# Attention of a hybrid block by whole patches: a ring for probabilities, four paired tables, first loads off ScalarE, output stored by patches

## The chip, the cores and the metric

The kernel runs on one core of a Trainium2 chip. The metric is the device time in microseconds; each kernel is run several times and the median is taken. TensorE (PE) multiplies matrices from SBUF into PSUM, VectorE (DVE), ScalarE (ACT) and GpSimd (POOL) work on tiles of 128 partitions, and loads and stores are DMA transfers. They are issued from the instruction queues of ScalarE, GpSimd and SyncE (SP); an engine that issues one is occupied for that time.

## The reference

One layer of a trunk: x of 2048 positions (a grid of 32 rows by 64 columns) and 1024 channels is normalised, shifted and scaled, projected once (`h @ w_in + b_in`) and split between two head groups; their outputs are concatenated and projected back.

```python
na_out = neighbourhood_attention(na_q, na_k, na_v, rpb) * jax.nn.silu(na_z)
...
ml_out = hm * jax.nn.silu(ml_z)
return jnp.concatenate([na_out, ml_out], axis=-1) @ w_out
...
h_res = h_res + gate[:, None, :] * y
return rmsnorm(h_res, final_norm_w).astype(x.dtype)
```

Neighbourhood attention has 8 heads of 64 channels. Each position of the grid attends to a window of 8 rows by 16 columns of keys, clipped at the border; a table of relative positions is added to the scores and keys outside the window are masked. The second group is an mLSTM of 4 heads in both directions; only its result is read by the part that the change touches. Everything is float32; matmuls are done as three products of high and low parts (hi x hi, lo x hi, hi x lo).

## The kernel before

The program has three stretches: the projection and convolution, then the passes of the mLSTM with the remaining column blocks of the projection as filler (matmuls into `pq`, L1046), and from about 930 us on the attention with the output projection. The last stretch is what the change touches. There PE's order is written out by hand: slots are emitted one after the other, and between their parts `pump(n)` takes n matmuls from a queue of filler, first the last `pq`, then the output projection (`y`, L1626) of a finished patch.

The grid is cut into 16 patches of 8 rows by 16 columns (128 queries). A unit is a patch and one channel block `ct` of two heads, so there are 64 units. A slot of the kernel before takes a pair of units: `scores` multiplies their queries by the keys of the patch's window (264 to 480 keys) into four PSUM banks (`pS`, L1538), adds the table and takes the row's minimum on VectorE (`mn`, L1546; the signs are turned), and ScalarE takes the exponential and its sum (L1547). `values` then multiplies the transposed probabilities of the pair in the slot before by the values (`pO`, L1581). `normalised` divides by the sums on VectorE (L1558). `turned` transposes on PE, in three or four pieces per head (`pT`, L1566, one PSUM buffer), and ScalarE copies the result to SBUF (`pt`, L1568), four times per slot. Fillers stand in front of the first and behind each transposition: 6, 5, 5, 4, 4 matmuls (8, 7, 7, 7, 7 in the first three slots).

When both pairs of a patch are through, its attention output, gated with z, and the mLSTM's part are split into a high and a low part for the output projection: `mixed` calls `mix_high` (a ScalarE copy, L1596) and `mix_low` (a VectorE subtraction, L1601), first for the mLSTM's half, then for the attention's. This is done in every other slot, behind the second and third transposition. The finished halves of y are added to the residual x on VectorE (L1631), squared and summed on ScalarE (L1633), and after a reciprocal root the row is scaled (L1668) and stored (L1669, issued from GpSimd). ScalarE and VectorE work strictly in the order of emission.

Loads: value rows of a patch (`v`, L1466, one DMA per grid row), z (L1476), the mLSTM's part (`wlo_a`/`whi_a`, L1483) and x (L1493) are issued from GpSimd; q (L1448), the tables (`tab`, L1510) and weights from SyncE. Of the first patch, v, z, the mLSTM's part and the third q are issued from ScalarE. There are two table tiles; the order of units within a patch is turned so that a table that fits the next patch too isn't loaded again. Probabilities live in four tiles (`pbuf`), transposed ones in four others (`pt`).

Of the kernel before, what the change touches and what calls it, by code (L numbers as in the profile page):

```python
# [58 lines left out]
class Kernel:  # L59
# [965 lines left out]
    def nq_gen(self):  # L1025
# [66 lines left out]
        while late:  # L1092
            nc.scalar.dma_start(*late.pop(0))
# [152 lines left out]
    def ml_pass2(self, ml, h):  # L1246
# [11 lines left out]
        def load_z(gi):  # L1258
            while ("mz", h, gi) not in self.zdone:
                self.pump(1)  # L1260
            if h == MH - 1 and gi == NG - 1:
                t = self.p2.tile([P, 4, P], F32, tag="pt", bufs=4, name="zt_last")
            else:
                t = self.mle.tile([P, 4, CH], F32, tag="zt", bufs=1, name=f"zt_{h}_{gi}")
# [134 lines left out]
    def phase2(self):  # L1399
# [23 lines left out]
        og = self.out[0].rearrange("(r c) d -> r c d", c=GRID_W)  # L1423
# [4 lines left out]
        qs = [p.tile([P, 2, 2, P], F32R, name=f"qs{i}") for i in range(3)]  # L1428
# [8 lines left out]
        units = []  # L1437
        for b in patches:
            again = units and kind(b) == kind(units[-1][0])
            order = range(4) if not units or not (again == (units[-1][1] == 3)) else range(3, -1, -1)  # L1440
            units += [(b, ct) for ct in order]
        NU = len(units)

        def load_q(i):
            if 2 * i >= NU:
                return
            b, c0 = units[2 * i][0], min(units[2 * i][1], units[2 * i + 1][1])
            (nc.gpsimd, nc.gpsimd, nc.scalar, nc.sync)[min(i, 3)].dma_start(qs[i % 3].bitcast(F32), self.d_qna[c0 // 2, b])  # L1448
# [48 lines left out]
        tabs = [p.tile([P, 960], F32, name=f"tab{i}") for i in range(2)]  # L1497
        place, follows, user = [], {}, {}
        for u, (b, ct) in enumerate(units):
            same = [w for w in (u - 1, u - 3) if w >= 0 and units[w][1] == ct and units[w][0] != b and kind(units[w][0]) == kind(b)]  # L1500
            place.append(place[same[0]] if same else (1 - place[u - 1] if u else 0))
            if not same:
                follows[user.get(place[u], -1 - place[u])] = u
            user[place[u]] = u

        def load_tab(u):
            b, ct = units[u]
            nk = geo[b][4]
            src = self.d_t[PR_T[b // 4]][PC_T[b % 4]][ct].rearrange("q e k -> q (e k)")
            (nc.gpsimd if u < 2 else nc.sync).dma_start(tabs[place[u]][:, : 2 * nk], src)  # L1510
# [11 lines left out]
        U = {}  # L1522

        def scores(pair):
            made = {}
            for u in pair:
                b, ct = units[u]
                pr, pc, nr, nkc, nk, rpc, nch = geo[b]
                q, c = qs[(u // 2) % 3], ct % 2
# [4 lines left out]
                for n, (e, f) in enumerate(((0, 0), (1, 0), (0, 1))):  # L1534
                    for j, ps in enumerate(made[u]):
                        js = slice(j * HD, (j + 1) * HD)
                        o = ps.rearrange("p (r c) -> p r c", c=nkc)
                        nc.tensor.matmul(o, q[js, e, c, :], keys[f][js], start=(n == 0), stop=(n == 2))  # L1538
            for u in pair:
                nk = geo[units[u][0]][4]  # L1540
                pts = []
                sums = few.tile([P, 2], F32, tag="sums", bufs=3, name=f"sums_{u}")
                for j, ps in enumerate(made[u]):
                    pt = pbuf[(2 * u + j) % 4]
                    mn = few.tile([P, 1], F32, tag="mn", bufs=4, name=f"mn_{u}_{j}")
                    nc.vector.tensor_tensor_reduce(pt[:, :nk], ps, tabs[place[u]][:, j * nk : (j + 1) * nk], 1.0, 3e38, ALU.add, ALU.min, mn)  # L1546
                    nc.scalar.activation(pt[:, :nk], pt[:, :nk], AF.Exp, bias=mn, scale=-1.0, accum_out=sums[:, j : j + 1])  # L1547
                    pts.append(pt)
                if u in follows:
                    load_tab(follows[u])  # L1550
# [10 lines left out]
        def turned(u, j):  # L1561
# [5 lines left out]
            t = p.tile([P, 4, P], F32, tag="pt", bufs=4, name=f"pt_{u}_{j}")  # L1567
# [3 lines left out]
        def values(pair):  # L1571
            po = pO.tile([P, 2, P], F32, tag="pO", name=f"pO_{pair[0]}")
            for u in pair:
# [3 lines left out]
                for i in range(nch):  # L1577
                    v, n = L[b]["v"][i]
                    for j in range(2):
                        h = 2 * ct + j  # L1580
                        nc.tensor.matmul(po[j * HD : (j + 1) * HD, ct % 2, :], v[:n, h * HD : (h + 1) * HD], pt[j][:n, i, :], start=(i == 0), stop=(i == nch - 1))  # L1581
            return po

        def gated(pair, po):
            b, ct = units[pair[0]]
            c0 = ct // 2 * 2
# [154 lines left out]
        def slot(m):  # L1741
            new = (2 * m, 2 * m + 1) if 2 * m < NU else ()
            old = (2 * m - 2, 2 * m - 1) if m else ()
            if m:
                load_q(m + 2)
# [139 lines left out]
```

## Time and profile before

| what | value |
|---|---|
| median of the runs shown | 1314.05 us (1313.41 to 1314.33) |
| profiled execution, its own time | 1315.58 us |
| its span, first to last instruction | 1313.8 us |
| PE busy | 1282.8 us, 98% |
| VectorE, ScalarE, GpSimd busy | 793.4, 531.3 and 260.6 us |
| first matmul of scores | about 950 us |
| last stores issued | 1306.04 and 1306.26 us |

The busy time of PE is modelled from pipelined records: a matmul that is shown 0.40 us long can be followed by the next one after 0.23 us. What PE spends is therefore read from start to start. In rows of the timeline stand the start, the duration, engine, line, operation, output and inputs, shapes and the number of records in a run, and in brackets how long the engine had been idle and what released it. In rows of waits stand who waited at which line for what, the sum in us, the number of times and the longest one. An engine name with a q is its queue, issuing a DMA.

### The profile page before, as it was taken

The numbers are of one execution on the slowest core, as the hardware profiler recorded it, in microseconds if no ns is written. First come the engines' busy times: TensorE is split into PE (matmuls) and PEld (weight loads), VectorE is DVE, ScalarE is ACT, GpSimd is POOL, SyncE is SP. The second block draws the span as 40 slices with busy tenths as digits, with TensorE's granted clock in tenths as the row PEclk, the third lists the DMA queues.
The fourth block names the chain that finished last, engine by engine and source line by source line (L and its number), as shares of the span: only waits on it lengthen the run. The fifth ranks groups of instructions, "written<-read, shape, count | busy, mean of one in ns | idle before, by whom it ended". The sixth has DMA issues, their size and how long they took to land.

```text
span 1313.8 us, 23067 instructions
## 1 busy us (share of the span) xinstructions
PE 1282.8 (98%) x8170; PEld 1103.1 (84%) x8170; DVE 793.4 (60%) x2394; ACT 531.3 (40%) x1172; POOL 260.6 (20%) x380
## 2 busy tenths in 40 slices
PE   9889999999999999999999999999999999999996
PEld 8889999999888887888888888888777778778785
DVE  5876452112567565166678878767447576766663
ACT  4444243542234222223323323333256555565551
POOL 1400002432000000111212002122305423324431
PEclk7989999999999999999999999999999999999998
DMA  9799955997778764645756767656678756656651
GB/s 363 250 282 305 262 188 152 228 234 202 195 183 186 170 149 110 193 131 165 207 153 209 245 184 215 214 157 183 206 252 261 203 182 194 209 181 194 190 178 48
DMA packets 220662, 263.31 MB, mean 200 GB/s; under 512 B 25463, under 2 KB 165623, under 8 KB 220548
## 3 DMA queue, kind: packets, MB, share of 16 engines
q1 hardware_dynamic: 142526, 189.92, 50.1%
q10 hardware_dynamic: 63270, 35.75, 9.6%
q0 software_dynamic: 14752, 36.17, 9.4%
q8 instruction: 65, 1.06, 0.3%
q14 instruction: 49, 0.40, 0.1%
HBM read 177.28 MB, written 92.72 MB: 206 GB/s over the span
## 4 chain that ended last, share of the span: by engine, by line
PE 80%; issue 4%; DVE 3%; DMA 3%; ACT 1%; POOL 1%; POOLq 0%; ACTq 0%; SPq 0%; DVEq 0%
PE pq L1046 23%; PE y L1626 11%; PE pc L605 4%; PE pc L606 4%; PE pc L604 4%; PE pO L1581 3%; PE pT L1566 3%; PE pvo L604 3%; PE pvo L606 3%; PE pvo L605 3%; PE pS L1538 2%; PE pv L606 2%; PE pv L605 2%; PE pv L604 2%; PE pi L1285 2%
## 5 line engine op out<-in xcount | busy, mean ns | idle before, releaser
L1046 PE MATMUL pq<-hhi,whi_a 128*128 128x512 f32 x512 | 208.4, 407 | 0.9 <-ACT u L951 0.9
L1046 PE MATMUL pq<-hlo,whi_a 128*128 128x512 f32 x512 | 208.2, 407 | 0.0
L1046 PE MATMUL pq<-hhi,wlo_a 128*128 128x512 f32 x512 | 206.7, 404 | 0.0
L1046 PEld LDWEIGHTS pq<-hhi,whi_a 128*128 128x128 f32 x512 | 96.8, 189 | 17.5 <-ACT u L951 1.3
L1046 PEld LDWEIGHTS pq<-hhi,wlo_a 128*128 128x128 f32 x512 | 96.7, 189 | 16.9 <-POOL wlo_a L1020 0.4
L1046 PEld LDWEIGHTS pq<-hlo,whi_a 128*128 128x128 f32 x512 | 96.8, 189 | 16.1 <-issue 0.5
L1020 POOL TENSOR_TENSOR wlo_a<-rawq,whi_a 128x1024 fp32r<-128x1024 f32 x19 | 45.6, 2399 | 293.3 <-ACT whi_a L1019 281.6
L1568 ACT ACTIVATE pt<-pT 96x384 f32<-96x384 f32 (+3 forms) x128 | 65.8, 514 | 87.3 <-PE pT L1566 85.1
L1547 ACT ACTIVATE pbuf<-pbuf,mn 128x480 f32<-128x480 f32 (+5 forms) x128 | 75.9, 594 | 47.8 <-DVE mn L1546 47.8
L1626 PE MATMUL y<-hhi,whi_a 128*128 128x512 f32 x256 | 91.6, 420 | 0.5 <-ACT whi_a L1596 0.5
L1626 PE MATMUL y<-hhi,wlo_a 128*128 128x512 f32 (+1 forms) x272 | 90.6, 399 | 0.2 <-ACT y L1633 0.2
L1466 POOL DMA_DIRECT2D v<-d_vna x158 | 81.8, 523 | 45.0 <-PE pO L1581 17.0
L1288 ACT ACTIVATE num<-px,gtile 128x129 f32<-128x129 f32 x120 | 38.3, 366 | 113.1 <-PE px L1283 80.4
L1546 DVE CUSTOM_DVE_ANT_0 pbuf<-pS,tab 128x480 f32<-128x480 f32 (+5 forms) x128 | 61.8, 539 | 32.3 <-PE pS L1538 32.3
L1307 POOL TENSOR_TENSOR hm<-hm,ck 128x128 f32<-128x128 f32 x64 | 27.5, 429 | 250.6 <-DVE hm L1306 218.5
L1566 PEld LDWEIGHTS pT<-ident,pbuf 128*128 128x128 f32 (+2 forms) x416 | 51.1, 136 | 23.2 <-ACT pt L1568 5.7
L1566 PE MATMUL pT<-ident,pbuf 128*128 128x128 f32 (+2 forms) x416 | 67.0, 274 | 3.0 <-DVE pbuf L1558 2.1
L604 PE MATMUL pvo<-whi_b,hhi 128*128 128x256 f32 x224 | 63.9, 285 | 0.7 <-DVE gates L678 0.7
L606 PE MATMUL pvo<-whi_b,hlo 128*128 128x256 f32 x224 | 63.1, 282 | 0.0
L605 PE MATMUL pvo<-wlo_b,hhi 128*128 128x256 f32 x224 | 63.1, 282 | 0.0
L893 ACT ACTIVATE dec<-dec,gtile 128x128 f32<-128x128 f32 x128 | 41.3, 391 | 49.2 <-POOL dec L886 46.4
L676 DVE TENSOR_TENSOR stvo<-pvo,brow 128x256 f32<-128x256 f32 x60 | 24.8, 419 | 57.6 <-PE pvo L606 44.9
(334 smaller groups left out, 3371.8 us busy)
## 6 DMA issues: line engine op xcount, KB each, us to landing
ck<-d_ck SPq DMA_DIRECT2D x64, 384.5 KB, 3.5
rawq<-in_w_main_dram SPq DMA_DIRECT2D x28, 512.0 KB, 4.5
raw<-in_w_main_dram SPq DMA_DIRECT2D x18, 512.0 KB, 6.1
kv<-d_ck SPq DMA_DIRECT2D x64, 128.5 KB, 2.8
dec<-d_mneg SPq DMA_DIRECT2D x32, 256.0 KB, 5.5
d_ck<-dec ACTq DMA_DIRECT2D x32, 256.0 KB, 7.2
d_qna<-qst ACTq DMA_DIRECT2D x32, 256.0 KB, 4.6
d_ck<-stvo SPq DMA_DIRECT2D x15, 514.0 KB, 4.8
```

The lines of the kernel that those rows point to most:

```text
L604: nc.tensor.matmul(ps, lhi(k), rhi(k), start=(k == 0), stop=False)
L605: nc.tensor.matmul(ps, lhi(k), rlo(k), start=False, stop=False)
L606: self.mark = nc.tensor.matmul(ps, llo(k), rhi(k), start=False, stop=(k == KT - 1))
L893: nc.scalar.activation(t[:, o, :], t[:, o, :], AF.Exp, bias=self.cols["g"][:, d, h, c : c + 1])
L1020: (eng or nc.gpsimd).tensor_tensor(lo[:, :, cs], raw, hi[:, :, cs].bitcast(F32), ALU.subtract)
L1046: self.mark = nc.tensor.matmul(patch_ps(ps) if patch else ps, w, self.htok(h, g, k, patch), start=(k == 0 and n == 0), stop=(k == KT - 1 a ...
L1466: queue.dma_start(chunks[key][r * nkc : (r + 1) * nkc, :], rows[r])
L1546: nc.vector.tensor_tensor_reduce(pt[:, :nk], ps, tabs[place[u]][:, j * nk : (j + 1) * nk], 1.0, 3e38, ALU.add, ALU.min, mn)
L1547: nc.scalar.activation(pt[:, :nk], pt[:, :nk], AF.Exp, bias=mn, scale=-1.0, accum_out=sums[:, j : j + 1])
L1566: nc.tensor.transpose(ps[:cs, i, :], U[u][j][:, i * cs : (i + 1) * cs], self.ident)
L1568: nc.scalar.activation(t[:cs, :nch, :], ps[:cs, :nch, :], AF.Copy)
L1626: nc.tensor.matmul(y, m[:, k, :], w[k][:, cs], start=(k == 4 and n == 0), stop=(k == 3 and n == 2))
```

## The change

A slot is now a whole patch, of four units; there are 16 slots and a last one for the remainder. In a slot, PE has the scores of the first two units, the values of all four units of the patch before, and the scores of the other two units, and after that eight transposes with 10, 5, 5, 5, 5, 5, 4, 4, 5 matmuls of filler before, between and behind them (10, 6, 6, 6, 6, 5, 4, 4, 9 in slot 2). `scores` is split: the adding of tables and the exponentials are a function of their own, `weights`. All probabilities and their transposes take turns in a ring of ten tiles, in place of the two sets of four. Each of the four channel blocks has a table tile of its own, which is loaded again only where the kind of patch changes (44 loads instead of 54), and the order of units is always 0 to 3. There are two tiles for q instead of three.

The copies for the output projection are made behind the fourth and fifth of the eight transposes (of a patch's first output projection earlier, in slot 2 and split around the scores). The value rows of a patch are loaded in the slot before they are used, two pieces, two and the rest behind the first, third and fifth transposition; z behind the second. The loads for the first patch that ScalarE issued are issued from GpSimd, and the last stores of q to DRAM from SyncE. The output is a tensor of 16 patches of 128 rows, stored as one block per patch and put in order outside the kernel. The scratch for software DMA is set to 4096 bytes.

On PE, from the first transposition of a pair's slot to the second one after the next scores, before (`pS` scores, `pO` values, `pT` transposes, `y` the output projection):

```order
L1566 MATMUL pT_1_11365<-ident,pbuf_9914 128x128 x4
L1626 MATMUL y_1_11232<-hhi_102,wlo_a 128x512 x2
L1626 MATMUL y_1_11232<-hlo_103,wlo_a 128x512
L1626 MATMUL y_1_11232<-hhi_102,wlo_a 128x512
L1538 MATMUL pS_0_11378<-hlo_1210,qs_9816 128x480
...
L1581 MATMUL pO_11408<-pt_0_11324,v_1_10952 64x128
...
L1581 MATMUL pO_11408<-pt_0_11351,v_1_10952 64x128
```

and with the change:

```order
L1611 MATMUL y_0_12108<-hlo_626,wlo_a 128x512
L1522 MATMUL pS_0_12136<-hhi_1209,qs_9814 128x480
...
L1522 MATMUL pS_0_12144<-hlo_1210,qs_9814 128x480
...
L1568 MATMUL pO_12152<-ring_9920,v_0_12051 64x128
...
L1522 MATMUL pS_0_12197<-hhi_906,qs_9815 128x480
...
L1522 MATMUL pS_1_12206<-hlo_907,qs_9815 128x480
L1611 MATMUL y_0_12108<-hhi_625,wlo_a 128x512 x2
```

Between two stretches of scores there are now only the values, without filler; the next filler comes behind the second scores.

On ScalarE, the copies of transposes (L1568) of one odd slot before with the output projection's work among them:

```order
L1568 ACTIVATE pt_0_12324<-pT_0_12319 128x512
L1568 ACTIVATE pt_1_12336<-pT_1_12331 128x512
L1596 ACTIVATE whi_a<-whi_a 128x512
L1568 ACTIVATE pt_0_12351<-pT_0_12346 128x512
L1633 ACTIVATE y_0_12187,fss_12185<-xr_12229 128x512
L1596 ACTIVATE whi_a<-zs 128x512
L1568 ACTIVATE pt_1_12370<-pT_1_12365 128x512
```

and the eight copies of one slot with the change (L1555):

```order
L1555 ACTIVATE ring_9916<-pT_0_12245 128x512
L1555 ACTIVATE ring_9917<-pT_1_12266 128x512
L1555 ACTIVATE ring_9918<-pT_0_12281 128x512
L1555 ACTIVATE ring_9919<-pT_1_12293 128x512
L1581 ACTIVATE whi_a<-whi_a 128x512
L1555 ACTIVATE ring_9920<-pT_0_12307 128x512
L1618 ACTIVATE y_0_12108,fss_12106<-xr_12129 128x512
L1581 ACTIVATE whi_a<-zs 128x512
L1555 ACTIVATE ring_9921<-pT_1_12321 128x512
L1555 ACTIVATE ring_9922<-pT_0_12332 128x512
L1618 ACTIVATE y_1_12238,fss_12106<-xr_12129 128x512
L1555 ACTIVATE ring_9923<-pT_1_12348 128x512
```

The chain of copy, square and copy that stood behind the slot's second copy, with one more copy to come, now stands behind the fourth, with the sixth, seventh and eighth to come.

On GpSimd's queue, the loads and the store of one patch before:

```order
L1669 DMA out_dram<-xr_11981 8x16x1024
L1483 DMA wlo_a<-d_mix 128x512
L1466 DMA v_1_12356<-d_vna 32x512 x4
L1466 DMA v_0_12450<-d_vna 32x512 x4
L1476 DMA zs<-d_zna 128x512
```

and with the change:

```order
L1653 DMA out_dram<-xr_11659 128x1024
L1470 DMA zs<-d_zna 128x512
L1477 DMA whi_a<-d_mix 128x512
L1460 DMA v_0_12051<-d_vna 32x512 x4
L1487 DMA xr_12129<-in_x_p_dram 128x1024
L1460 DMA v_1_12251<-d_vna 32x512 x4
L1460 DMA v_0_12256<-d_vna 32x512 x4
L1653 DMA out_dram<-xr_11891 128x1024
```

The last piece of v (here `v_0_12051`) stands behind the store, the load of z and that of the mLSTM's part, and it is read by the values of the next slot.

The diff, cut to its core (the lines that only rename or move a tile are left out):

```diff
         while late:
-            nc.scalar.dma_start(*late.pop(0))
+            nc.sync.dma_start(*late.pop(0))
...
-        tabs = [p.tile([P, 960], F32, name=f"tab{i}") for i in range(2)]
...
+        tabs = [p.tile([P, 960], F32, name=f"tab{i}") for i in range(4)]
...
-            pt = pbuf[(2 * u + j) % 4]
+            pt = turn()
...
-        def values(pair):
-            po = pO.tile([P, 2, P], F32, tag="pO", name=f"pO_{pair[0]}")
+        def values(us):
+            po = pO.tile([P, 4, P], F32, tag="pO", name=f"pO_{us[0]}")
...
-            to = og[8 * pr : 8 * pr + 8, 16 * pc : 16 * pc + 16, :]
+            to = self.out[b]
...
+        ring += [p.tile([P, 512], F32, name=f"ring_{i}") for i in range(3, 10)]
+        for t in ring:
             nc.vector.memset(t, 0.0)
+        order = itertools.cycle(ring)
+        turn = lambda: next(order)
...
         extra = {
-            (0, -1): [lambda: load_v(b0, 4, nc.scalar), lambda: load_z(b0, nc.scalar), lambda: load_q(2)],
-            (0, 2): [lambda: nc.scalar.dma_start(m0, self.d_mix[b0]), lambda: load_z(b1)],
...
+            (0, -1): [lambda: load_v(b0), lambda: load_z(b0)],
+            (0, 4): [lambda: nc.gpsimd.dma_start(m0, self.d_mix[b0])],
...
+        def loads(b, n):
+            m = pos[b]
+            if n in (2, 5) and m + 1 < len(patches):
+                load_q(2 * m + 2 + (n == 5))
+            if m and n in (0, 2, 4):
+                load_v(b, 4 if n == 4 else 2)
+            if m and n == 1:
+                load_z(b)
...
+            if b is not None:
+                scores(us[:2])
             if m:
+                po = values(range(4 * m - 4, 4 * m))
...
+            weights(us[:2])
...
+            for u in us[:2]:
+                normalised(u)
+            if m == 0:
+                self.pump(12)
+            scores(us[2:])
+            weights(us[2:])
+            if m:
+                gated(prev, po)
+            for u in us[2:]:
+                normalised(u)
...
+            at = 4 if m == 2 else 3
+            fills = (10, 6, 6, 6, 6, 5, 4, 4, 9) if m == 2 else (10, 5, 5, 5, 5, 5, 4, 4, 5)
+            for n in range(-1, 8):
                 if n >= 0:
+                    turned(us[n // 2], n % 2)
                     if n % 2:
                         step()
                     finish()
+                    if m > 1 and n in (at, at + 1):
+                        mixed(prev, n % 2)
+                    loads(b, n)
...
-_OUTS = [((1, 2048, 1024), 'float32')]
+_OUTS = [((16, 128, 1024), 'float32')]
...
-    nc = _bacc.Bacc("TRN2", target_bir_lowering=False, num_devices=1)
+    nc = _bacc.Bacc("TRN2", target_bir_lowering=False, num_devices=1, dynamic_dma_scratch_size=4096)
...
+    return r.results[0]["out_0_dram"].reshape(4, 4, 8, 16, D).transpose(0, 2, 1, 3, 4).reshape(1, T, D)
```

More of the change, by code (lines that the diff above doesn't have):

```diff
@@ L1426, in phase2 @@
         fnw = []
-        qs = [p.tile([P, 2, 2, P], F32R, name=f"qs{i}") for i in range(3)]
+        qs = [p.tile([P, 2, 2, P], F32R, name=f"qs{i}") for i in range(2)]
         zs = [p.tile([P, 4, P], F32, name="zs"), self.gtile[:, 0:4]]
@@ L1434, in kind @@
             return PR_T[b // 4], PC_T[b % 4]
[L1437 to L1441, printed above, removed]
+        units = [(b, ct) for b in patches for ct in range(4)]
         NU = len(units)
```

147 lines of the change are left out of this document (56 added, 91 removed).

## The prediction, made before the changed kernel was run

> **What bounds the kernel now.** I read the head of the page first, then the stretch from 930 us on that the change touches, as a table by stage, and then the waits of TensorE (PE) in its first part.
>
> ```profile
> span 1313.8 us, 23067 instructions
> PE 1282.8 (98%) x8170; PEld 1103.1 (84%) x8170; DVE 793.4 (60%) x2394; ACT 531.3 (40%) x1172; POOL 260.6 (20%) x380
> ...
> 930.00:976.00 46.00, 44.42 (x238) 34.74 (x238) 18.36 (x54) 18.59 (x39) 9.66 (x19) 1.00 0.82 261
> 976.00:1003.00 27.00, 24.64 (x167) 19.20 (x163) 19.17 (x42) 18.55 (x36) 12.38 (x24) 0.94 0.85 276
> 1003.00:1022.00 19.00, 18.81 (x138) 14.72 (x136) 14.11 (x46) 11.16 (x30) 6.99 (x13) 1.00 0.65 182
> 1022.00:1290.00 268.00, 268.00 (x2014) 214.03 (x2013) 177.14 (x589) 149.55 (x394) 91.17 (x170) 1.00 0.63 189
> ...
> PE pT L1566 <- DVE pbuf L1558: 2.1, 2, 1.9
> PE pT L1566 <- ACT pt L1568: 0.9, 1, 0.9
> PE ht L1339 <- ACT hm L1332: 0.5, 1, 0.5
> PE y L1626 <- ACT whi_a L1596: 0.5, 1, 0.5
> ```
>
> The table's columns are the window, its length, the busy time of PE, weight loads, VectorE (DVE), ScalarE (ACT) and GpSimd (POOL), then PE's granted clock, the DMA share and GB/s. PE is the bound: from 1022 to 1290 us it is busy for all of 268.00 us at clock 1.00. Nothing that other engines do faster can pay there; only PE's own sequence can get shorter, and a new wait can make it longer. From 930 to 1003 us PE waits (the last four rows): 4.0 us in five waits, the longest 1.9 us, and behind it the clock falls:
>
> ```profile
> 994.00:995.00 1.00, 0.13 (x1) 0.16 (x2) 0.96 (x6) 1.00 (x4) 0.00 (x0) 1.00 1.07 411
> 995.00:996.00 1.00, 1.00 (x6) 0.88 (x6) 0.96 (x5) 0.82 (x4) 0.55 (x1) 0.81 1.04 399
> 996.00:997.00 1.00, 1.00 (x3) 0.61 (x3) 0.36 (x2) 0.86 (x1) 0.07 (x1) 0.50 1.04 307
> 998.00:999.00 1.00, 1.00 (x4) 0.73 (x3) 0.12 (x1) 1.00 (x2) 1.00 (x3) 0.50 0.53 200
> ```
>
> The microsecond between the two rows of 0.50 has 0.50 too, so 0.19 + 3 x 0.50 = 1.7 us of PE time are lost to the clock.
>
> **Term 1, the switches between kinds of matmul: -3.2 us.** One slot of the kernel before, on PE:
>
> ```profile
> 1113.39 0.40 PE L1626 MATMUL y<-hlo,wlo_a 128*128 128x512 f32 x1
> 1113.62 0.40 PE L1626 MATMUL y<-hhi,wlo_a 128*128 128x512 f32 x1
> 1113.95 0.80 PE L1538 MATMUL pS<-hhi,qs 64*128 64x384 f32 x6
> ...
> 1115.22 1.53 PE L1581 MATMUL pO<-pt,v 128*64 128x128 f32 x24
> 1116.68 0.50 PE L1626 MATMUL y<-hhi,whi_a 128*128 128x512 f32 x1
> 1117.02 0.39 PE L1626 MATMUL y<-hlo,whi_a 128*128 128x512 f32 x1
> ...
> 1123.76 0.80 PE L1538 MATMUL pS<-hlo,qs 64*128 64x384 f32 x6
> ...
> 1188.04 1.98 PE L1581 MATMUL pO<-pt,v 128*64 128x128 f32 x32
> ```
>
> One y follows another after 0.23 us (1113.39 to 1113.62). The step from y to scores (pS) takes 0.33, so 0.10 more; the first y after pO takes 0.34 (1116.68 to 1117.02), so 0.11 more. The eight pO records that 32 have over 24 cost 1.98 - 1.53 = 0.45, or 0.056 each; 24 of them make 1.35, and pO lasts 1.46 from start to start, so about 0.11 is the entry from pS to pO; A slot of a pair has three switches, 0.32; two slots, that is one patch, 0.64. A slot of a whole patch has y to pS, pS to pO, pO to pS, pS to y: 0.10 + 0.11 + x + 0.11, where x, from pO back to pS, stands nowhere in this trace; it lies between 0 and 0.11. I take 0.11, since every change of kind that the trace shows costs about that. That saves 0.64 - 0.43 = 0.21 per patch, in 15 patches (the first has no values to compute) 3.2 us; with x at 0 it is 4.8. The transposes keep their number and their fills, and the count of y, pS and pO matmuls is the same.
>
> **Term 2, the start: -3.6 us.** Before loses 4.0 us in waits and 1.7 by the clock. A y record is 0.40 long and the next starts after 0.23, so each of the five waits hides 0.17 more: 0.9. Sum 6.6. One of them is ScalarE's queue:
>
> ```profile
> 956.54 0.49 ACT L1568 ACTIVATE pt<-pT 96x384 f32<-96x384 f32 x1 [2.18 <-DMA v<-d_vna]
> ...
> 957.72 1.29 ACTq L1049 DMA_DIRECT2D d_qna<-qst  x2
> L1022 ACT ACTIVATE whi_a<-rawq x8: 1050/1060/1063, 727.2 to 959.1; 128x1024 fp32r<-128x1024 f32 x8
> ```
>
> The first copy waits 2.18 us behind the loads that ScalarE issues. The change issues these on POOL, which has them first in its order, and the next work that ScalarE has there is late instead: in the new slot 0 its order is eight exponentials, two issues of d_qna (1.29), one split of L1022 (1.06), then the first copy. The last exponential ends about 2.3 us after the second scores (four adds and exponentials of the second pair, pipelined), so the first copy ends at 2.3 + 1.29 + 1.06 + 0.5 = 5.1; the second transpose would come after ten and five fills at 0.1 + 10 x 0.23 + 1.5 = 3.9. I count 1.2 us there. In slot 1 I count 0.25, and in slot 2, where ScalarE has an eviction and VectorE splits, an eviction and a mix subtraction ahead of the first copy and where the second scores wait for VectorE to free their PSUM banks, 1.5. Together 3.0, so 3.6 of the 6.6 are won. Bounds: 1.0 if only the queue of slot 0 shows (won 5.6), 6.1 if the three places behave like the hole of before (won 0.5).
>
> **Term 3, the tail: -1.7 us.** The last two stores are issued at 1306.04 and 1306.26, and the span ends at 1313.8; they carry 256 KB each.
>
> ```profile
> 1306.26 0.69 ACTq L1660 DMA_DIRECT2D out_dram<-xr  x1
> ...
> 1272.00:1273.00 1.00, 1.00 (x8) 0.81 (x7) 0.76 (x2) 0.60 (x2) 0.18 (x1) 1.00 0.97 352
> 1309.00:1310.00 1.00, 0.00 (x0) 0.00 (x0) 0.00 (x0) 0.00 (x0) 0.00 (x0) 0.50 0.51 186
> 1310.00:1311.00 1.00, 0.00 (x0) 0.00 (x0) 0.00 (x0) 0.00 (x0) 0.00 (x0) 0.50 0.47 182
> ```
>
> While they move, half of the DMA engines' time is used (0.51 and 0.47, at 186 GB/s), though loads reach 0.97 and 352. The destination before is 8 grid rows of 16 columns; the change makes it one block of 128 rows. If the moving goes at the higher rate, 512 KB take 1.5 us instead of 2.8, and the last piece's start may improve too: 0 to 2.4, I take 1.7. [...]
>
> **Term 4, a new wait of TensorE in every patch: +4.9 us.** This is what speaks against the change. The copies of the transposed probabilities (L1568) share ScalarE with the copy for the output projection (mix_high, L1596) and the square (L1633), and the square waits for VectorE's add, which stands behind mix_low. Before, in the odd slots:
>
> ```profile
> 1109.86 0.49 PE L1566 MATMUL pT<-ident,pbuf 128*128 128x128 f32 x3
> ...
> 1110.83 0.62 ACT L1596 ACTIVATE whi_a<-whi_a 128x512 fp32r<-128x512 f32 x1
> ...
> 1111.49 0.69 DVE L1601 TENSOR_TENSOR whi_a<-whi_a 128x512 fp32r<-128x512 f32 x1 [2.86 <-ACT whi_a L1596]
> 1112.10 0.68 DVE L1631 TENSOR_TENSOR xr<-xr,y 128x512 f32<-128x512 f32 x1
> ...
> 1112.81 0.60 ACT L1633 ACTIVATE y<-xr 128x512 f32<-128x512 f32 x1 [0.38 <-DMA v<-d_vna]
> ...
> 1113.44 0.61 ACT L1596 ACTIVATE whi_a<-zs 128x512 fp32r<-128x512 f32 x1
> 1113.96 0.47 ACT L1568 ACTIVATE pt<-pT 128x384 f32<-128x384 f32 x1
> ```
>
> From the transpose at 1109.86 the chain runs to a copy that ends at 1114.43, 4.57 us later. There it is the slot's last copy, the next work on PE is scores and values for which it is not needed at once, so PE does not wait. In the changed order the same chain begins behind the fourth of eight transposes, and the copy at its end is the sixth, which frees the one PSUM buffer for the seventh. Transposes with five y between them lie 1.49 apart, with four 1.25 (the first is 0.25 + 0.31 + 4 x 0.23 and some rounding), so the seventh comes 1.49 + 1.49 + 1.25 = 4.23 behind the fourth. PE waits 4.57 + 0.04 - 4.23 = 0.38 us (0.04 is what mix_low takes to follow mix_high's end, 1110.83 + 0.62 to 1111.49). Slots 3 to 15 have it: 13 x 0.38 = 4.9. Bounds: 0, if ScalarE reaches it sooner; 7, at 0.55 each.
>
> **Costed small.** The patch's value rows are now loaded in the slot before their use, with the last of them behind the store of the finished patch in POOL's order; of these:
>
> ```profile
> out_dram<-xr POOLq DMA_DIRECT2D x15, 512.0 KB, 6.8
> v<-d_vna POOLq DMA_DIRECT2D x94, 48.0 KB, 5.0
> v<-d_vna POOLq DMA_DIRECT2D x64, 64.0 KB, 6.4
> ...
> POOL out_dram L1669 <- DVE xr L1668: 80.5, 13, 10.4
> ```
>
> A slot of a pair takes 9.8 us (1113.95 to 1123.76), one of a patch some 20. The store waits for VectorE behind the second transpose, about 10.6 us into the slot (two scores of 1.27, values of 2.8, twenty y and two transposes); behind it stand loads of z, of the mix part and the last four or five v, of 0.5 us issue each, so the last v is issued at about 14.2 and lands 5.0 to 6.4 later, at 20.6 at most; the values need it at 20.2 to 21. I put 0.3 us for all slots, with 0 and 8 as bounds (seven slots have a chunk there that late; 1.2 each if it lands 1.5 us later). The tables (four, each reloaded only where the kind of patch changes, 44 loads for 54) and the q loads are on the sync queue and a slot ahead of their use. The ten ring tiles replace eight and are cleared by six more memsets on VectorE while PE works on pq. The smaller scratch for software DMA I cost at nothing: the waits of POOL's loads that this trace shows are on transfers that were issued eight earlier.
>
> **The sum.** -3.2 - 3.6 - 1.7 + 4.9 + 0.3 = -3.3. The profiled execution took 1315.58 us with a span of 1313.8; its own would become 1312.3 with a span of 1310.5. The median of the runs stands 1.5 below that execution: 1314.05 - 3.3 = 1310.8.
>
> **The rivals.**
>
> A, no wait behind the chain. If ScalarE gets through mix and square before the seventh transpose, term 4 is 0. For it speaks that PE waits for no such copy from 1022 to 1290 now; against it that the new order puts the chain ahead of two more transposes. Time: 1314.05 - 8.2 = 1305.8.
>
> B, the start gains nothing. Slots 0 to 2 are dense on ScalarE and VectorE (18.55 and 19.17 of 27 us in the second row of the table); one hole of 2 us, as at 994, brings the half clock with it, 1.7 us more. Then term 2 is 0: 1314.4. [...]
>
> C, slower: the v loads. The place is pO of the next patch, the price 1.2 us in each of seven slots, 8.4 in all, and it decides once the last v lands more than some 6.5 us behind its issue. For it speaks the 6.4 of the 64 KB loads, against it that a store now leaves the queues sooner. Time: 1310.8 - 0.3 + 8.4 = 1318.9.
>
> D, it does not do what it says: PE's switches do not get cheaper, as a change from pO back to pS may cost more than 0.11. At 0.32 term 1 is 0, and the time is 1314.0, which lies with B.
>
> **How the numbers follow.** The forecast has 0.45 (its own range 1308.5 to 1313), A 0.20, B with D 0.20, C 0.15. A measurement of this kernel can tell about 0.2%, 2.6 us, from no change: faster is below 1311.4, slower above 1316.7. The forecast gives about 0.30 faster and 0.15 the same, A 0.20 faster, B and D 0.17 the same and 0.03 slower, C 0.15 slower: 0.50, 0.32, 0.18. The range 1305 to 1317 holds all but C and a little beyond A.
>
> **What would show it.** In the waits of PE from 1030 to 1290, a row of pT on ScalarE's copy of about 13 times and 5 us shows term 4; no row shows A. A row of pO on v shows C. On the timeline the eight transposes of a patch should lie 1.49 or 1.25 apart but for the seventh, at 1.6. The DMA share behind 1307 should be near 1 and the span end 1.7 us sooner after the last issue. PE's waits from 930 to 1003 should be about 3 us with no row of clock 0.50; a 0.50 there shows B. The forecast is wrong in sign if pO waits, and in size if the seventh transpose does not.

## The result and the profile after

The changed kernel takes 1304.99 us (median; 1303.76 to 1305.46) beside 1314.19 us before (1313.41 to 1316.21): a ratio of 0.9919, with a 95% interval of 0.9898 to 0.9939, so 9.2 us faster. That is almost three times the forecast gain of 3.3 us, 0.8 us under the time that rival A gave and just under the lower end of the range.

The head of the page of the changed kernel, the table by stage (columns as in the prediction), and PE's waits before and after 1030 us:

```profile
span 1303.7 us, 22944 instructions
PE 1277.4 (98%) x8170; PEld 1103.3 (85%) x8170; DVE 794.7 (61%) x2384; ACT 532.3 (41%) x1172; POOL 258.6 (20%) x385
...
930.00:976.00 46.00, 45.02 (x272) 35.54 (x271) 23.99 (x78) 20.98 (x51) 11.25 (x21) 1.00 0.88 268
976.00:1003.00 27.00, 26.42 (x183) 21.40 (x182) 20.71 (x49) 20.89 (x45) 11.27 (x22) 1.00 0.88 281
1022.00:1280.00 258.00, 255.68 (x1932) 206.13 (x1930) 169.95 (x546) 143.83 (x373) 87.37 (x171) 1.00 0.55 172
...
PE pT L1553 <- ACT ring L1555: 1.7, 3, 1.0
PE y L1611 <- ACT y L1618: 0.4, 1, 0.4
...
PE pT L1553 <- ACT ring L1555: 2.1, 12, 0.2
PE y L1611 <- ACT y L1618: 0.2, 1, 0.2
```

Two things are to be seen. PE is no longer without a gap between 1022 and 1280 us: it waits 12 times for ScalarE's copy, as term 4 said, so rival A, which shares the time, is not what happened. And the clock stays at 1.00 in the stage where it had fallen. No row of pO on v is there, so rival C did not come.

To see where the 10.1 us between the two profiles went, I cut both executions at three points that both programs share: the last matmul of the mLSTM (`pi`), the last y, and the issue of the last store.

```profile
925.85 0.61 PE L1285 MATMUL pi<-ck 128*128 128x129 f32 x4
...
1302.00 0.28 PE L1626 MATMUL y<-hhi,wlo_a 128*128 128x256 f32 x1
```

```profile
924.32 0.61 PE L1285 MATMUL pi<-ck 128*128 128x129 f32 x4
...
1296.01 0.28 PE L1611 MATMUL y<-hhi,wlo_a 128*128 128x256 f32 x1
...
1300.27 0.36 ACTq L1644 DMA_DIRECT2D out_dram<-xr  x1
```

| stretch, us | before | after | difference |
|---|---|---|---|
| start to last `pi` | 925.9 | 924.3 | -1.5 |
| last `pi` to last y | 376.2 | 371.7 | -4.5 |
| last y to last store's issue | 4.3 | 4.3 | 0 |
| that issue to the end | 7.5 | 3.4 | -4.1 |

I do not count the first row as a gain of the change. In the profiles of all runs here it lies between 923.0 and 927.9 but for one, and the six profiles with the order of the kernel before spread from 923.5 to 927.6; the first transposes at the very beginning start between 14.1 and 19.6 us. This spread at the start makes single executions of one kernel differ by several us (1311.98 to 1318.89 for the kernel before on the chip of the first four experiments). So the experiments below are read by the stretches inside their profiles, and the medians stand beside them.

One slot in the steady part, on PE (compare the slot of a pair in the prediction):

```profile
1112.47 0.80 PE L1522 MATMUL pS<-hhi,qs 64*128 64x384 f32 x6
...
1113.73 2.84 PE L1568 MATMUL pO<-ring,v 128*64 128x128 f32 x48
1116.50 0.80 PE L1522 MATMUL pS<-hhi,qs 64*128 64x384 f32 x6
...
1124.63 0.49 PE L1553 MATMUL pT<-ident,ring 128*128 128x128 f32 x3
...
1129.20 0.55 PE L1553 MATMUL pT<-ident,ring 128*128 128x128 f32 x3 [0.18 <-ACT ring L1555]
...
1132.08 0.93 PE L1522 MATMUL pS<-hhi,qs 64*128 64x480 f32 x6
```

The slot takes 19.61 us (1112.47 to 1132.08), two slots of a pair took 2 x 9.81 = 19.62. But the seventh transposition comes 4.57 us behind the fourth, where 4.23 would do: 0.34 us are a wait (0.18 of it beyond the modelled end of the y ahead). So the new order saves about 0.33 us per patch and the new wait takes it all back; in the steady part nothing is won. (4.23 is an estimate from the spacing of the other transpositions; the run with the copies two earlier, below, measures both sizes without it.)

At the end, the moving of the last store, and what SyncE waited for last, after and then before:

```profile
1301.00:1302.00 1.00, 0.00 (x0) 0.00 (x0) 0.00 (x0) 0.00 (x0) 0.00 (x0) 0.50 1.02 385
...
SPq L1877 <- DMA out_dram<-xr: 1.9, 2, 1.3
SPq L1877 <- PEq L1877: 0.7, 2, 0.5
```

```profile
1307.00:1308.00 1.00, 0.00 (x0) 0.00 (x0) 0.00 (x0) 0.00 (x0) 0.00 (x0) 0.50 0.39 47
1308.00:1309.00 1.00, 0.00 (x0) 0.00 (x0) 0.00 (x0) 0.00 (x0) 0.00 (x0) 0.50 0.42 109
...
SPq L1881 <- DMA out_dram<-xr: 4.3, 2, 3.0
SPq L1881 <- PEq L1881: 2.0, 2, 1.5
```

The block moves at a share of 1.02 and 385 GB/s instead of 0.51 and 186. The move before was also slower at its start than the rows in the prediction show: it goes at 47 and 109 GB/s in its first two microseconds and takes some 3.7 us (1307.25 to 1311.0), and the new one some 1.5. Besides, the end before waits 1.5 us for TensorE's queue (PEq), behind the store; after, it waits 0.5. The prediction had not looked at that row.

### The profile page after: what moved, and what is told of

Read it like the earlier page. It is cut to its first block, busy times and chain, and to the rows that moved or that the text cites. A ratio compares the mean times of both kernels' runs of the same rounds, so it can differ in the third digit from the quotient of the medians.

```text
span 1303.7 us, 22944 instructions
## 1 busy us (share of the span) xinstructions
PE 1277.4 (98%) x8170; PEld 1103.3 (85%) x8170; DVE 794.7 (61%) x2384; ACT 532.3 (41%) x1172; POOL 258.6 (20%) x385
## 4 chain that ended last, share of the span: by engine, by line
PE 77%; issue 5%; ACT 3%; DVE 3%; DMA 2%; POOL 1%; POOLq 0%; SPq 0%; ACTq 0%; DVEq 0%
PE pq L1046 24%; PE y L1611 7%; PE pc L605 4%; PE pc L606 4%; PE pc L604 4%; PE pvo L604 3%; PE pvo L606 3%; PE pvo L605 3%; PE pO L1568 3%; PE pT L1553 2%; PE pv L606 2%; PE pv L605 2%; PE pv L604 2%; PE pS L1522 2%; PE pi L1285 2%
## 5 line engine op out<-in xcount | busy, mean ns | idle before, releaser
L1534 ACT ACTIVATE ring<-ring,mn 128x480 f32<-128x480 f32 (+5 forms) x128 | 76.0, 595 | 56.9 <-DVE mn L1533 56.6
L1555 ACT ACTIVATE ring<-pT 96x384 f32<-96x384 f32 (+3 forms) x128 | 65.6, 513 | 64.1 <-PE pT L1553 62.3
L1611 PE MATMUL y<-hhi,whi_a 128*128 128x512 f32 x256 | 88.6, 410 | 0.0
L1460 POOL DMA_DIRECT2D v<-d_vna x158 | 79.0, 506 | 26.0 <-DMA v<-d_vna 6.3
L1553 PEld LDWEIGHTS pT<-ident,ring 128*128 128x128 f32 (+2 forms) x416 | 50.4, 136 | 26.9 <-ACT ring L1555 12.3
L1553 PE MATMUL pT<-ident,ring 128*128 128x128 f32 (+2 forms) x416 | 67.0, 274 | 3.9 <-ACT ring L1555 3.9
L1533 DVE CUSTOM_DVE_ANT_0 ring<-pS,tab 128x480 f32<-128x480 f32 (+5 forms) x128 | 62.4, 540 | 7.1 <-PE pS L1522 6.0
```

The costliest lines, as they stand in the source:

```text
L1460: queue.dma_start(chunks[key][r * nkc : (r + 1) * nkc, :], rows[r])
L1533: nc.vector.tensor_tensor_reduce(pt[:, :nk], ps, tabs[ct][:, j * nk : (j + 1) * nk], 1.0, 3e38, ALU.add, ALU.min, mn)
L1553: nc.tensor.transpose(ps[:cs, i, :], U[u][j][:, i * cs : (i + 1) * cs], self.ident)
L1555: nc.scalar.activation(t[:cs, :nch, :], ps[:cs, :nch, :], AF.Copy)
L1611: nc.tensor.matmul(y, m[:, k, :], w[k][:, cs], start=(k == 4 and n == 0), stop=(k == 3 and n == 2))
```

## The experiments

**Output by grid rows again, in the changed kernel.**

```diff
-            to = self.out[b]
+            pr, pc = divmod(b, 4)
+            to = og[8 * pr : 8 * pr + 8, 16 * pc : 16 * pc + 16, :]
...
```

> The changed kernel with the output stored as before, by grid rows of 16 columns (the destination's outer dimension is 8 again); all else as changed. Theory: the tail from the last store's issue to the end goes back from 3.4 to 7.5 us, and nothing else on PE moves, so 1305.0 + 4.1 = 1309.1 us, with the 15 other stores landing after some 6.8 us again instead of 3.0. Rival 1 (the prediction's term 3): only half of the moving time comes back, +1.7, so 1306.7. Rival 2: the longer stores keep GpSimd's queue back and the last v of a patch comes late, so PE waits at pO in some slots and the time is 1311 or more.

Measured: 1308.85 us, ratio to before 0.9962 (0.9947 to 0.9978). The stretch from the last issue to the end is 6.0 us, not 7.5: the store costs 2.6 of the 4.1 us, and SyncE's last waits are

```profile
SPq L1879 <- DMA out_dram<-xr: 4.2, 2, 3.0
SPq L1879 <- PEq L1879: 0.7, 2, 0.5
...
PE pO L1569 <- DMA v<-d_vna: 1.2, 3, 0.8
```

so the wait for TensorE's queue did not come back with the layout. The last row is rival C on a small scale: with stores that land after 7.2 us instead of 3.0, the last v of three patches is late, and `pi` to last y takes 372.5 instead of 371.7. The mechanism was there; the shorter store had taken it away.

**Output by patches alone, in the kernel before.**

```diff
-            pr, pc = divmod(b, 4)
-            to = og[8 * pr : 8 * pr + 8, 16 * pc : 16 * pc + 16, :]
+            to = self.out[b]
...
```

> The kernel before with the output stored by patches, nothing else. Theory: the tail from the last issue to the end falls from 7.5 to 3.4 us, so 1314.2 - 4.1 = 1310.1, with a DMA share near 1 while the last block moves. Rival (the prediction's term 3): 1314.2 - 1.7 = 1312.5.

Measured: 1315.54 us, ratio 1.0010 (0.9991 to 1.0029): nothing, though the store moved in 1.6 us.

```profile
1305.00:1306.00 1.00, 0.00 (x0) 0.00 (x0) 0.00 (x0) 0.00 (x0) 0.00 (x0) 0.50 0.99 375
...
SPq L1879 <- PEq L1879: 4.7, 2, 4.2
SPq L1879 <- DMA out_dram<-xr: 1.9, 2, 1.3
```

What the store gave, the wait for TensorE's queue took: 4.2 us instead of 1.5. In both kernels the end comes 11.7 to 11.8 us after the last y (1313.8 - 1302.0 and 1311.5 - 1299.8). My expectation of -4.1 was wrong.

**The small scratch alone, in the kernel before.**

```diff
-    nc = _bacc.Bacc("TRN2", target_bir_lowering=False, num_devices=1)
+    nc = _bacc.Bacc("TRN2", target_bir_lowering=False, num_devices=1, dynamic_dma_scratch_size=4096)
```

> The kernel before with the scratch for software DMA at 4096 bytes, nothing else. In the profiles the changed kernel is 1.5 us ahead already at about 903 us, where its program has not been changed. Theory: this is the spread of loads at the start, and the time is that of before, 1314.2. Rival: the smaller scratch makes the start or the software DMA quicker, 1312.7; or its ring fills up and POOL waits: 1315 or more.

Measured: 1315.01 us, ratio 0.9996 (0.9978 to 1.0013), no difference that the runs can tell. But the wait for TensorE's queue is 0.5 in its profile, and the end comes 10.4 us after the last y, some 1.3 us sooner than before: now the slow store is what ends last. In this profile the hole of the fourth slot (TensorE idle for 1.90 us) is there, but the clock stays at 1.00 behind it, and `pi` to last y takes 374.6 instead of 376.2:

```profile
992.47 0.52 PE L1566 MATMUL pT<-ident,pbuf 128*120 128x128 f32 x3 [1.90 <-DVE pbuf L1558]
...
994.00:995.00 1.00, 1.00 (x7) 0.88 (x6) 0.51 (x1) 0.95 (x3) 0.20 (x1) 1.00 1.07 341
```

**The kernel before once more.**

> The kernel before, a second profile. In its first one, and in that of the kernel before with output by patches, the end came 11.7 us after the last y, with SyncE waiting last for TensorE's queue (1.5 and 4.2 us); in all profiles of kernels with the scratch of 4096 bytes that wait is 0.5. Theory: the wait for TensorE's queue belongs to the larger scratch and repeats: 11.7 us again. Rival: it varies from execution to execution: another value here, as small as 10.4.

The theory held: 1.5 us of wait for TensorE's queue, 11.7 us from the last y to the end (1314.9 - 1303.2).

**Output by patches and small scratch together, in the kernel before.**

> The kernel before with the output stored by patches and the scratch at 4096 bytes, nothing else. Theory: output by patches saves 2.7 us between the last issue and the end, but the kernel before hides it behind the wait for TensorE's queue, which only the smaller scratch takes away: together 7.7 us from the last y to the end instead of 11.7, and a median some 3 to 4 us under that of before, where each alone gave nothing. Rival: the two do nothing together either: the median is that of before, and the wait for TensorE's queue shows again.

Measured: 1310.93 us, ratio 0.9974 (0.9962 to 0.9986), 3.4 us less, where neither part alone moved the median. From the last y to the end it takes 7.7 us, against 11.7 with the new store alone and 10.4 with the small scratch alone. Two things ended within some 1.3 us of each other, and only taking both away shows in full. Over all profiles of this study, the four with the larger scratch have a longest wait of 1.5 to 4.2 us for TensorE's queue at the end, the twelve with 4096 bytes have 0.5. Why TensorE's queue ends later with the larger scratch no run shows; that stays open.

**The last store with an outer dimension of 8, and of 4, in the changed kernel.**

```diff
-            to = self.out[b]
+            to = self.out[b].rearrange("(p a) d -> a p d", a=8) if end else self.out[b]
...
```

The second run has `a=4` in the same place.

> The changed kernel with the last patch's two stores given an outer dimension of 8 (rows of the patch in another order in memory, so the last patch's rows are permuted in the output; each row is 2 KB as before). Theory: the outer dimension sets how many DMA engines a store uses; 8 of 16, a share of 0.5 while it moves and 2.7 us more from the last issue to the end, 3.4 to 6.1. Rival: it was the spread of the rows over the whole output, in 8 groups far apart, that made it slow: 3.4 us as in the changed kernel.

> As the run with an outer dimension of 8, but 4. Theory: 4 of 16 engines, a share of 0.25, the moving time doubles once more (3.5 to about 6 us): 8.5 to 10 us from the last issue to the end. Rival: no difference from the run with 8.

One microsecond of the moving, with 8 and with 4:

```profile
1307.00:1308.00 1.00, 0.00 (x0) 0.00 (x0) 0.00 (x0) 0.00 (x0) 0.00 (x0) 0.50 0.51 195
```

```profile
1304.00:1305.00 1.00, 0.00 (x0) 0.00 (x0) 0.00 (x0) 0.00 (x0) 0.00 (x0) 0.50 0.26 100
```

From the last issue to the end: 6.1 and 9.3 us, beside 3.4 with 128. The rows are as long as before and lie inside one block of 512 KB, so it is the outer dimension, not the spread over the output: with 8 of it the store uses half of the 16 DMA engines' time while it moves (0.51), with 4 a quarter (0.26), and with 128 all of it (1.02). The rows give this share, not how many of the engines take part.

**The copies for the output projection two transpositions later, in the changed kernel.**

```diff
-            at = 4 if m == 2 else 3
+            at = 4 if m == 2 else 5
```

> The changed kernel with the copies for the output projection behind the sixth and seventh transposition instead of the fourth and fifth (from the fourth slot on). Theory: the wait of 0.33 us ahead of the seventh transposition, in 13 slots, goes away, since ScalarE's square of the first half no longer stands behind mix_low, and the last copy is needed only by the next slot's values: 13 x 0.33 = 4.3 us, so 1300.7. Rival 1: by the waits of the profile only 2.1 us are lost there, so 1302.9. Rival 2: the wait moves to the output projection's matmuls behind the seventh transposition, which now need the new high and low parts at once (they are made about 0.2 us ahead): 1304 to 1305, with a row of y on mix_low.

Measured: 1309.65 us, ratio to before 0.9965 (0.9948 to 0.9982): 4.7 us slower than the changed kernel; `pi` to last y takes 376.2. The wait at the seventh transposition is gone, and a larger one stands at the second:

```profile
PE pT L1553 <- ACT ring L1555: 6.4, 10, 1.2
...
1030.02 0.16 DVE L1391 TENSOR_TENSOR frs<-frs,nwt_f 128x1 f32<-128x1 f32 x1
1030.14 0.53 DVE L1533 CUSTOM_DVE_ANT_0 ring<-pS,tab 128x352 f32<-128x352 f32 x1
...
1036.96 0.47 ACT L1555 ACTIVATE ring<-pT 128x384 f32<-128x384 f32 x1
...
1037.49 0.55 PE L1553 MATMUL pT<-ident,ring 128*128 128x128 f32 x3 [0.65 <-ACT ring L1555]
```

The square of the second half of y now stands behind both copies, so its reciprocal root on VectorE (which ends with L1391) comes late, and the table adds of the next slot (L1533) stand behind it in VectorE's order: the first begins 2.57 us behind the start of the slot's scores (1027.57), where the changed kernel has 1.19 (1112.47 to 1113.66). From there it goes through the exponentials, the divisions and the second pair's adds to the first copy, which ends 0.6 us too late. In the changed kernel the same first copy ends at 1121.29 and the second transposition starts at 1121.67: 0.38 us to spare. I had looked at the chain that I moved and not at what stands behind it in the next slot; theory and both rivals fell.

**The copies two transpositions earlier.** The same line with `else 1`. It ran beside the changed kernel on the same chip.

> The changed kernel unchanged, on the chip of the next three, as their measure. Theory: from the last mLSTM matmul to the last y it takes 371.7 us as in its first profile (376.2 before), with about twelve waits of the seventh transposition of 0.2 us each by the waits, and 3.4 us from the last store's issue to the end plus what the end waits for TensorE's queue.

> The changed kernel with the copies for the output projection behind the second and third transposition (from the fourth slot on) instead of the fourth and fifth. VectorE's adds and ScalarE's squares of y stay where they were, so no copy of a transposition stands behind the chain of mix_high, mix_low, add and square any more, and the square of the second half, whose reciprocal root stands ahead of the next slot's table adds on VectorE, is no later than in the changed kernel. Theory: the 13 waits of 0.33 us at the seventh transposition go, 4.3 us from the last mLSTM matmul to the last y (371.7 to 367.4). Rival 1: as with the copies two later, a wait of about the same size opens at the second transposition, whose predecessor's copy has 0.4 us to spare in the changed kernel: 371 to 376. Rival 2: the mLSTM's part has not landed when it is copied that early, and the wait is at the third transposition.

Measured: 1298.29 us (1297.38 to 1298.85), ratio to before 0.9868 (0.9853 to 0.9882), beside 1306.49 us (1304.13 to 1308.38) and 0.9930 (0.9911 to 0.9947) for the changed kernel. `pi` to last y takes 366.0 us instead of 371.1. PE's waits behind 920 us in that run of the changed kernel:

```profile
PE pT L1553 <- ACT ring L1555: 3.3, 15, 0.6
PE y L1611 <- ACT y L1618: 0.6, 2, 0.4
```

and with the copies earlier:

```profile
PE pT L1553 <- ACT ring L1555: 0.9, 2, 0.6
PE y L1611 <- ACT y L1618: 0.6, 2, 0.4
```

13 of the 15 waits are gone, with 5.2 us of PE's time, where 4.3 were expected. This is term 4, measured by taking away what makes it wait, and it is the fastest version of the study, under both kernels. The same slot as above, from scores to scores:

```profile
1108.87 0.81 PE L1522 MATMUL pS<-hhi,qs 64*128 64x384 f32 x6
...
1128.08 0.93 PE L1522 MATMUL pS<-hhi,qs 64*128 64x480 f32 x6
```

It takes 19.21 us, 0.40 less than the 19.61 with the wait. The twelve slots from the fourth patch's scores to the last patch's take 242.6 us before (1021.80 to 1264.42), 243.0 with the change (1010.42 to 1253.42) and 238.3 here (1008.79 to 1247.06). So the new order saves 4.3 us there, 0.36 per patch, and the wait costs 4.7, 0.39 per patch, more than the change wins there. The medians lie 8.2 us apart; what goes beyond 5.2 I do not put down to the edit, since the start alone moves single executions by several us (the last `pi` lies between 923.5 and 927.6 in the six profiles with the order of the kernel before).

**And the stores of q from SyncE in addition.**

```diff
-                            nc.scalar.dma_start(*late.pop(0))
+                            (nc.sync if kind == "q" else nc.scalar).dma_start(*late.pop(0))
```

> As the run with the copies two earlier, and the stores of q to DRAM issued from SyncE instead of ScalarE. Theory: the wait ahead of the second transposition of the first slot (1.13 us from start to start) is ScalarE's two issues of 1.29 us ahead of the first copy; it goes, 1.1 us less than the run with the copies two earlier alone. Rival: the split of weights (1.06 us), which stands there too, still keeps the copy back by some 0.2 us, or SyncE's queue brings the q loads of the first slots later and PE waits at the scores: no gain or a loss of 1 to 3.

Measured: 1302.27 us, ratio 0.9907 (0.9888 to 0.9925), slower than without. `pi` to last y is 366.5, so the first slot wins nothing (its wait is 0.32 us, as in the run without), and the last `pi` comes at 931.0 instead of 923.3. How much of that is the spread of the start and how much the q stores in SyncE's queue during the mLSTM is not settled.

**One y between values and second scores.**

```diff
+            elif m > 3:
+                self.pump(1)
             scores(us[2:])
...
-                self.pump(fills[n + 1])
+                self.pump(fills[n + 1] - (1 if n < 0 and m > 3 else 0))
```

> The changed kernel with one y of the ten behind the second scores moved to between the values and the second scores, from the fifth slot on (12 slots). This brings back two switches of kind, values to y and y to scores, 0.11 + 0.10, in place of the direct one from values to scores. Theory (the direct one costs nothing): 12 x 0.2 = 2.5 us more from the last mLSTM matmul to the last y, 371.7 to 374.2. Rival (the prediction's, 0.11 for the direct one): 1.2 us more. Rival 2: switches cost nothing when the order is fixed by the program, and the gain came from elsewhere: 371.7.

Measured: 1307.81 us, ratio to before 0.9950 (0.9933 to 0.9968); `pi` to last y 373.1 instead of 371.1, so 2.0 us for 12 slots, 0.165 each. Two switches of together 0.21 less a direct one make 0.165, so the direct one costs about 0.05 on average, between the two ends of the prediction and nearer to nothing. The average mixes two kinds of slots: of the eleven that can be read from scores to scores, nine take 0.19 to 0.23 us more than in the changed kernel, and two take 0.02 and 0.08 more. In the nine the direct switch is left with about nothing, as the theory had it; why the two gain less is not shown.

**The first loads on ScalarE again, in the changed kernel, and off it in the kernel before.**

```diff
-            (0, -1): [lambda: load_v(b0), lambda: load_z(b0)],
+            (0, -1): [lambda: load_v(b0, 4, nc.scalar), lambda: load_z(b0, nc.scalar)],
-            (0, 4): [lambda: nc.gpsimd.dma_start(m0, self.d_mix[b0])],
+            (0, 4): [lambda: nc.scalar.dma_start(m0, self.d_mix[b0])],
```

> The changed kernel with the first patch's v, z and mLSTM part issued from ScalarE again (five issues of 0.4 to 0.6 us), all else as changed. Theory: ScalarE has them ahead of the first slot's work, the second transposition of the first slot waits some 2 us longer and from the last mLSTM matmul to the last y it takes 373 instead of 371.3. Rival: in the changed order ScalarE's exponentials are late anyway and hide the issues: 371.3.

Measured: 1312.41 us, ratio to before 0.9988 (0.9971 to 1.0005): four fifths of the change's gain are gone. `pi` to last y takes 377.7.

```profile
958.91 3.34 ACTq L1049 DMA_DIRECT2D d_qna<-qst  x2
...
963.78 0.88 PE L1553 MATMUL pT<-ident,ring 128*96 128x128 f32 x3 [5.41 <-ACT ring L1555]
...
964.00:965.00 1.00, 1.00 (x5) 0.89 (x5) 0.61 (x1) 0.31 (x1) 0.00 (x0) 0.50 0.26 100
966.00:967.00 1.00, 1.00 (x4) 0.67 (x4) 0.00 (x0) 0.00 (x0) 0.00 (x0) 0.50 0.27 102
```

Four of the loads go ahead of the two stores of q on ScalarE's queue. The stores then take 3.34 us to issue, where the changed kernel has 0.41 and 1.15 and the kernel before 1.29. PE waits 5.41 us, with the half clock behind it. I expected 2 us. Why the stores take longer no run shows: in the kernel before they also came after the loads, but 1.2 us later.

> The kernel before with these loads and the third q issued from GpSimd, and the last stores of q from SyncE, as in the change, nothing else. Theory: only the wait of 1.1 us at the first slot's second transposition goes; the hole of 1.9 us at the fourth slot, with the half clock behind it, stays, since it comes from VectorE's splits of weights: 375.3 instead of 376.4 from the last mLSTM matmul to the last y. Rival: the loads on ScalarE set off the hole too, and 4 us or more go.

Measured: 1311.29 us, ratio 0.9973 (0.9956 to 0.9990), 3.0 us less; `pi` to last y 372.5 instead of 376.2 to 377.5. The rival's size came true, 3.7 to 5.0 us, but not its mechanism. The wait of the first slot's second transposition goes (0.95 us and more in the kernel before) and so does one of 0.48 of y on mix_high. The hole of the fourth slot is still there, 1.50 us instead of 1.9, and a later one grows from 0.19 to 0.46; the clock stays up:

```profile
992.83 0.52 PE L1566 MATMUL pT<-ident,pbuf 128*120 128x128 f32 x3 [1.50 <-DVE pbuf L1558]
...
994.00:995.00 1.00, 1.00 (x8) 0.82 (x7) 0.32 (x2) 0.90 (x2) 0.51 (x1) 1.00 1.03 403
```

That the clock stays up is worth some 1.5 us (376.2 against 374.6), and it is not shown to come from the loads: it stayed up as well in the profile with the small scratch alone, with the loads on ScalarE and a hole of 1.90 us. Against that profile's 374.6, 2.2 us are left for the loads. The end comes 12.3 us after the last y here, with a last wait of 1.7 us for TensorE's queue.

## Why the prediction was right and wrong

The sign was right, the mechanism it feared was there, and the size was wrong: -9.2 instead of -3.3.

**Term 1** (-3.2): right in kind, too small. The new order saves 0.33 to 0.36 per patch instead of 0.21; 15 x 0.36 = 5.4, beyond the bound of 4.8. The step that failed is the choice of x = 0.11, "since every change of kind that the trace shows costs about that"; the run with one y between puts it at 0.05 on average and at about nothing in most slots. With x at 0 the working gives 0.32; what makes up the rest is not shown.

**Term 2** (-3.6): about right. The changed kernel's waits in its start are 1.7 + 0.4 us, and four of them with 0.17 hidden each make 2.8, where the prediction counted 3.0, with 1.13 us from start to start at the first slot's second transposition, where it counted 1.2. So 6.6 - 2.8 = 3.8 are won (4.4 in the second profile, whose three waits are 1.1 us together). What it had not seen is how much hangs on the loads on ScalarE: put back into the changed kernel they cost 6 us with the half clock, while taken off the kernel before they give some 2 us, and some 4 together with the clock that stayed up. The hole of the fourth slot is gone only with the new order; with the loads off alone 1.50 us of it stay.

**Term 3** (-1.7, bounds 0 to 2.4): the step that failed most. The stretch behind the last issue fell by 4.1 us. Of this 2.6 to 2.7 belong to the outer dimension of the store (6.0 or 6.1 against 3.4 us), a little more than the upper bound of 2.4. The prediction took 2.8 us for the old move, at the 186 GB/s of its later rows; the trace of before has 3.7, because its first two microseconds go at 47 and 109. That the new store would move at the 352 GB/s of the loads was an estimate that the trace of before does not show; in the changed kernel it moved at 385. The new move takes the 1.5 that it allowed, and starts 0.5 us behind its issue instead of 1.0. The other 1.4 belong to an edit costed at nothing, "the smaller scratch for software DMA": I looked for it in POOL's waits, and it shows in the last wait of the program, SyncE's for TensorE's queue. Without it the store's gain would not have shown at all, as the kernel before with the new store alone tells.

**Term 4** (+4.9): right in place, mechanism and size. At the seventh transposition 0.34 us a slot were read from the spacing and 0.39 from the slots with the cause taken away, for 0.38 predicted; 13 x 0.39 = 5.1, and the whole stretch became 5.2 shorter.

**The v loads** (+0.3): 0. They land in time because the new store leaves the queues after 3.0 us; with the old store three patches waited, 1.2 us in all.

With the measured sizes, -5.4 - 3.8 - 4.1 + 5.1 = -8.2, against -9.2 between the medians and -8.6 between the two profiles without their first row; 0.4 us stay unassigned. So the steps that made the forecast too small are terms 3 and 1; the other two held. **Rival A** had the right time by accident: the wait that it denied is in the profile. **Rival B** did not happen: the half clock is gone. **Rival D** is excluded by the slot. As for the clock, it fell to 0.50 behind holes of 1.88 to 1.90 us in four profiles with the order of the kernel before, and stayed at 1.00 behind one of 1.90 in another, so the length of the hole alone does not decide it here.

## What to carry to other kernels

Look at the last wait of the program, not only at the last transfer: where two things end close together, shortening one of them alone can give nothing. Here the new store and the small scratch had ratios of 1.0010 and 0.9996 alone, and together they took 3.4 us off. When work is moved within a fixed order, follow what stands behind it in every queue into the next round: two places later cost 4.5 to 5.1 us of TensorE's time (376.2 against 371.7 and 371.1) and two earlier gave 5.2, with the same instructions. And keep transfers off the queue of an engine that a dense stretch waits for: in the changed kernel four loads of 0.5 to 0.7 us to issue each, and the stores behind them, made TensorE wait 5.4 us, with the half clock behind it.

## What the runs showed that was not expected

The size of the scratch for software DMA changed how late TensorE's queue ends (a last wait of 0.5 us in twelve profiles with 4096 bytes, 1.5 to 4.2 in four without); the cause is open. Two stores of q that take 0.41 and 1.15 us to issue in the changed kernel take 3.34 directly behind four loads on the same queue. And the clock can fall by half behind a hole of 1.9 us, but does not each time.
